# Residue-ordered keys and value rows, all attention scores in 64 by 32 tiles, far keys one block later

## The chip, the cores and the metric

The kernel runs on one core of a Trainium2 chip. The metric is device time in microseconds (us): the median of three runs of the kernel before is 1187.13 us (1186.64 to 1187.44). One further execution was taken by the hardware profiler; its own time is 1186.35 us, and the span from its first to its last instruction is 1184.6 us.

The engines are named as in the profile: PE (matrix products), PEld (PE's loading of the stationary operand), DVE (vector), ACT (activations, copies), POOL (general), SP (issues most DMAs). SBUF is the on-chip memory of 128 partitions, PSUM the memory that PE writes.

## The reference, cut to what matters

The computation is one layer of a decoder, 1024 positions by 1024 features, in float32. An input projection feeds 8 attention heads of 64 features and 4 gated-recurrence heads; their joined output is projected and added; a gated MLP with a short convolution follows, and a last norm. The change touches the attention alone, which is three causal dilated windows whose softmax sums are merged:

```python
DILATED_PATTERNS = ((128, 1), (512, 4), (2048, 16))   # (window, dilation), n_keys = window // dilation = 128
...
valid = (dist >= 0) & (dist <= n_keys) & (blk * ATTN_BLOCK + kj - ATTN_BLOCK >= 0)   # dist counted in dilated steps
s = jnp.where(valid[None, :, None, None], s, -jnp.inf)
p = jnp.exp(s - m[..., None]); l = jnp.sum(p, axis=-1)
...
w = jnp.exp(ms - jnp.max(ms, axis=0, keepdims=True))
den = jnp.sum(w * ls, axis=0); num = jnp.sum(w[..., None] * os_, axis=0)
return (num / den[..., None])[:, :S]
```

Since the three branches share scores, a query at position i sees key j with weight c(i-j) exp(score), where c counts the branches that allow the distance: every distance up to 128, multiples of 4 up to 512, multiples of 16 up to 2048. An additive mask with log c (or a very large negative number) in front of one softmax gives the same result. Two facts shape the kernel: beyond a distance of 128 only keys with the query's own residue modulo 4 count, since every multiple of 16 is one of 4 too; within it, any key may count.

## The kernel before, in words

The sequence is cut into 8 blocks of 128 queries, `b` = 0 to 7, and the 8 heads into 4 pairs, `p`; a pair's two heads `e` lie on partitions 0-63 and 64-127. `qp` and `kp` hold queries and keys with the feature on the partition. `qk_half` writes them from PSUM (lines 570 and 571): the queries of each block in the order of their residue r modulo 4 (32 queries of residue 0, then 32 of residue 1, and so on), the keys in their natural order.

`scores(p, b)` (lines 600 to 627) computes, for each of the two heads, one PSUM bank with 128 query rows. Its last columns are the near keys: the block itself and the block before it, 256 keys (128 for b = 0), as one matmul per head with 64 feature rows and 128 queries in the stationary operand (line 610). Its first `32 * b` columns are far keys: for each residue r a matmul with 32 stationary queries (line 615) that reads every fourth key from the start of the sequence to the end of block b - 1, each key 16 bytes after the last. So the previous block's own-residue keys stand in both parts, and the mask splits the distances between them. These matmuls are in plain float32; the profile shows each as two MATMUL records, so that two matmuls per near part are "x4" and eight per far part "x16". A transpose is one record.

DVE adds the mask and takes the row minimum of the negated scores (line 622), ACT takes the exponential and the row sum (line 624), DVE the reciprocal (line 625), POOL scales the probabilities (line 626). `turn(p, b)` (lines 631 to 656) transposes them on PE: `Tn` holds the near part (line 641, copied by ACT at line 642), `Tf` the far part, in one or two pieces of 128 columns (line 649, copied by DVE into `far_t` and `tri`, lines 653 and 656). `values(p, hf)` (lines 658 to 678) multiplies half a sequence (4 blocks) of transposed probabilities with the values: near with `V` (line 669), and per residue with the far rows, a full 128 keys from `far_t` (line 674) and up to 96 keys from `tri` (line 676).

The values come out of `tok` and `two` in natural order, position on the partition. `v_evac` (line 586) scales each block of 128 positions from PSUM straight into `V` and writes it to a buffer `vd` in DRAM as well (line 587); `load_far` (line 596) reads the residue-ordered far rows back.

PE's order is the program's own, written by hand. Between the pieces of attention, `fill.run` plays matmuls of the projections (lines 460 to 463, 477 to 479, 494 to 496, 514 to 516) by a fixed credit of us, so a block is: scores of the next block, filling, turn of this block, filling. The other engines' order and the DMA queues' come from a scheduler. Weights come through a ring (`Ring`): SP loads a raw chunk (line 66 or 253), ACT rounds its high part (line 86), POOL or DVE takes the rest (line 88), and up to five raw and five split chunks are ahead of PE.

Of the kernel before, what the change touches and what calls it, by code (L numbers as in the profile page):

```python
# [10 lines left out]
F32 = mybir.dt.float32  # L11
# [6 lines left out]
P = 128  # L18
# [5 lines left out]
DH = 64  # L24
# [178 lines left out]
def hybrid_kernel(ctx: ExitStack, tc: tile.TileContext, xT, w_qk, w_tok, w_hg, w_out, w_up,  # L203
# [322 lines left out]
    raw = {}  # L526
    iv = None
    if True:
        FAR, NEAR = 224, 256
        nat = at.tile([P, SEQ], F32, tag="k0", name="nat", bufs=2)  # L530
        sel = at.tile([P, FAR + NEAR], F32, tag="P0", name="sel", bufs=2)
        mask = at.tile([P, FAR + NEAR], F32, name="mask")
        scratch = drv.tile([P, FAR + NEAR], F32, name="scratch")
        nat1 = at.tile([P, FAR + NEAR], F32, tag="P1", name="nat1", bufs=2)
        nc.sync.dma_start(nat1[:, 0:NEAR], amask[:, SEQ - NEAR :])
        nc.sync.dma_start(nat[0:32, 0:896], amask[0:P:4, 0:896])
        NO = -8.0 * BIG

        POOL.tensor_scalar(sel[:, FAR:], nat1[:, 0:NEAR], DH ** 0.5, 0.0, op0=ALU.mult, op1=ALU.add)
        POOL.affine_select(out=sel[:, FAR:], in_=sel[:, FAR:], compare_op=ALU.is_ge, fill=NO, base=0,  # L540
                           pattern=[[1, NEAR]], channel_multiplier=-1)
        POOL.tensor_scalar(sel[0:32, 0:FAR], nat[0:32, 0:896:4], DH ** 0.5, 0.0, op0=ALU.mult, op1=ALU.add)
        POOL.affine_select(out=sel[0:32, 0:FAR], in_=sel[0:32, 0:FAR], compare_op=ALU.is_gt, fill=NO, base=192,
                           pattern=[[-1, FAR]], channel_multiplier=1)
        nc.sync.dma_start(scratch[:, FAR:], sel[:, FAR:])
        nc.sync.dma_start(scratch[0:32, 0:FAR], sel[0:32, 0:FAR])
        for r in range(4):
            nc.sync.dma_start(mask[32 * r : 32 * r + 32, FAR:], scratch[r:P:4, FAR:])
            nc.sync.dma_start(mask[32 * r : 32 * r + 32, 0:FAR], scratch[0:32, 0:FAR])

        tri = [at.tile([P, 2, 3, P], F32, name=f"tri{i}") for i in range(2)]
        for t in tri:
            POOL.memset(t, 0.0)
        for v, n, inv in ((V_AG, 4, 1.0 / 512), (V_HG, 4, 1.0 / P), (V_G2, 8, 1.0 / DM), (V_GF, 8, 1.0 / DM)):
            pin(POOL.tensor_scalar(vec[:, v : v + n], vec[:, v : v + n], -0.5 * inv, 0.0, op0=ALU.mult, op1=ALU.add))
        qk = {}

        def by_residue(ap):
            return ap.rearrange("p (b l r) -> p b r l", l=32, r=4)

        def qk_half(h, hf, last, tag="mm"):
            t = halves[hf]
            p, r0 = h // 2, 64 * (h % 2)

            def evac(ps):
                if p not in qk:
                    qk[p] = [at.tile([P, SEQ], F32, tag=x, name=f"{x}{p}", bufs=2) for x in ("qp", "kp")]
                qp, kp = qk[p]
                q4 = qp[r0 : r0 + 64, t].rearrange("p (b r l) -> p b r l", r=4, l=32)
                DVE.tensor_mul(q4, by_residue(ps[0:64]), by_residue(R1[0:64, t]))  # L570
                DVE.tensor_mul(kp[r0 : r0 + 64, t], ps[64:128], R1[64:128, t])
            return dense(("qk", h), hf, evac, last, tag)

        def qk_block(h):
# [5 lines left out]
        def v_evac(g):  # L580
            def evac(t, ps):
                nonlocal V
                if V is None:
                    V = vtile([P, 8, NH, DH], F32, "V")
                dst = V[:, t, 4 * g : 4 * g + 4]
                ACT.mul(dst, ps[:, :256].rearrange("p (h e) -> p h e", h=4), R1T[:, t : t + 1])
                nc.scalar.dma_start(vd[t * P : (t + 1) * P, 256 * g : 256 * g + 256], dst)
            return evac

        far_v = {}  # L590
# [9 lines left out]
        def scores(p, b):  # L600

            qp, kp = qk[p]
            far = 32 * b
            near = P if b == 0 else 2 * P
            k0 = (b + 1) * P - near
            n = far + near
            S = [bank("s", f"S{p}_{b}_{e}") for e in range(2)]
            rows = [slice(64 * e, 64 * e + 64) for e in range(2)]
            for e in range(2):
                PE.matmul(S[e][:, far:n], qp[rows[e], b * P : (b + 1) * P], kp[rows[e], k0 : k0 + near],  # L610
                          start=True, stop=True)
            for r in range(4 if b else 0):
                o = slice(32 * r, 32 * r + 32)
                for e in range(2):
                    PE.matmul(S[e][o, 0:far], qp[rows[e], b * P + 32 * r : b * P + 32 * r + 32],  # L615
                              kp[rows[e], r : r + 4 * far : 4], start=True, stop=True)
            m = mask[:, FAR - far :] if b else mask[:, FAR + P :]
            Ps = probs[p, b] = []
            for e in range(2):
                Pt = at.tile([P, FAR + NEAR], F32, tag=f"P{e}", name=f"P{p}_{b}_{e}", bufs=2)  # L620
                st = at.tile([P, 16], F32, tag="st", name=f"st{p}_{b}_{e}", bufs=8)
                DVE.tensor_tensor_reduce(Pt[:, :n], S[e][:, :n], m, -(DH ** -0.5), BIG * 3,  # L622
                                         op0=ALU.add, op1=ALU.min, accum_out=st[:, 0:1])
                ACT.activation(Pt[:, :n], Pt[:, :n], AF.Exp, bias=st[:, 0:1], scale=-1.0, accum_out=st[:, 2:3])  # L624
                DVE.reciprocal(st[:, 3:4], st[:, 2:3])  # L625
                POOL.tensor_scalar(Pt[:, :n], Pt[:, :n], st[:, 3:4], 1.0, op0=ALU.mult, op1=ALU.mult)  # L626
                Ps.append(Pt)

        near_t, far_t = {}, {}

        def turn(p, b):

            Ps = probs.pop((p, b))
            far = 32 * b
            T = bank("t", f"Tn{p}_{b}").rearrange("p (e x q) -> p e x q", e=2, x=2)
            d = near_t[p, b] = at.tile([P, 2, 2, P], F32, tag="pl", name=f"pl{p}_{b}", bufs=5)
            x0 = 0 if b else 1
            for e in range(2):
                for x in range(x0, 2):
                    c = far + (x - x0) * P  # L640
                    PE.transpose(T[:, e, x], Ps[e][:, c : c + P], ident)
            ACT.copy(d[:, :, x0:], T[:, :, x0:])
            if not b:
                return
            T = bank("t", f"Tf{p}_{b}").rearrange("p (x e q) -> p x e q", e=2, x=2)
            parts = 1 + (b > 4)
            for x in range(parts):
                for e in range(2):
                    PE.transpose(T[:, x, e], Ps[e][:, x * P : (x + 1) * P], ident)
            if b == 4:  # L650
                far_t[p] = at.tile([P, 2, 4, P], F32, tag="k0", name=f"k0_{p}", bufs=2)
            if b >= 4:
                DVE.tensor_copy(far_t[p][:, :, b - 4], T[:, 0])
            if b != 4:
                n = 32 * (b % 4)
                DVE.tensor_copy(tri[b // 4][0:n, :, b % 4 - 1], T[0:n, parts - 1])

        def values(p, hf):

# [10 lines left out]
            for r in range(4):  # L670
                q = slice(32 * r, 32 * r + 32)
                if hf:
                    for e in range(2):
                        PE.matmul(O4[rows[e], :, q], v[:, 0, r, rows[e]], far_t[p][:, e, :, q], start=False, stop=False)
                for e in range(2):
                    PE.matmul(O4[rows[e], 1:, q], v[0:96, hf, r, rows[e]], tri[hf][0:96, e, :, q], start=False, stop=(r == 3))
            DVE.tensor_copy(raw[p, hf].rearrange("p (b l r) -> p b l r", l=32, r=4),
                            O.rearrange("p (b r l) -> p b l r", r=4, l=32))

# [857 lines left out]
```

## Time and profile before

| | before |
|---|---|
| median of 3 runs | 1187.13 us |
| profiled execution, its own time | 1186.35 us |
| its span | 1184.6 us |
| PE busy | 1174.0 us, 6422 matmul records |
| DVE, ACT, POOL busy | 866.8, 563.3, 277.1 us |
| mean granted PE clock | 0.998 |
| the stretch with the attention, 36 to 265 us | 229 us, PE busy 228.94 |

A row of the page's groups reads: line, engine, operation, output<-inputs, shapes, count, then busy us and mean ns. A row of the timeline reads: start us, length us, engine, line, operation, tiles, the tile shape of PE (rows * columns of the stationary operand), partitions x columns that stream, count of records merged into the row. Consecutive records overlap in PE's pipeline, so what a group costs is read from its start to the start of the next group, not from its length.

### The profile page before, as it was taken

The page shows a single profiled execution, that of the slowest core. Times are in us where ns is not written, and L with a number is a line of the kernel's source. Part 1 is how long each engine was busy: PE and PEld are TensorE (multiplying, and loading weights), DVE is VectorE, ACT ScalarE, POOL GpSimd, SP SyncE. Part 2 cuts the span into 40 slices and gives each one's busy share as a digit, 9 for nine tenths or more (in the row PEclk, how much of TensorE's full clock was granted, in tenths as well). Part 3 has the DMA queues.
Part 4 walks back from the last instruction along what each step waited for, and adds up shares of the span by engine and source line. Part 5 has one row for each costly group of instructions (what it writes and reads, how often), then busy time and mean ns, then how long its engine had stood idle before and what let it go on. Part 6 is the DMA issues. An engine that isn't in the chain of part 4 may idle for free.

```text
span 1184.6 us, 17883 instructions
## 1 busy us (share of the span) xinstructions
PE 1174.0 (99%) x6422; PEld 964.1 (81%) x6422; DVE 866.8 (73%) x1585; ACT 563.3 (48%) x1103; POOL 277.1 (23%) x244
## 2 busy tenths in 40 slices
PE   9999999999999999999999999999999999999996
PEld 7978787778888888888888888888888888888886
DVE  7543434235887774567998988989888878858987
ACT  8424343566666655446434334343343444444553
POOL 1125253761101035231233122232222200000000
PEclk9999999999999999999999999999999999999999
DMA  7223040332112113440213332233323277435522
GB/s 259 82 76 117 28 125 28 110 121 85 37 37 81 54 63 125 142 141 29 72 54 125 116 111 85 98 125 116 107 73 113 92 241 253 140 96 168 167 94 95
DMA packets 78985, 126.73 MB, mean 107 GB/s; under 512 B 7920, under 2 KB 25104, under 8 KB 78896
## 3 DMA queue, kind: packets, MB, share of 16 engines
q1 hardware_dynamic: 65376, 103.63, 28.0%
q10 hardware_dynamic: 13520, 21.96, 4.9%
q8 instruction: 50, 0.82, 0.3%
q14 instruction: 39, 0.32, 0.1%
HBM read 99.71 MB, written 25.85 MB: 106 GB/s over the span
## 4 chain that ended last, share of the span: by engine, by line
PE 98%; DVE 1%; DMA 0%; POOL 0%; ACT 0%; SPq 0%; issue 0%; DVEq 0%; POOLq 0%
PE p L1136 11%; PE p L1137 11%; PE p L1138 11%; PE ds L1437 3%; PE ds L1435 3%; PE ds L1436 3%; PE po L1040 2%; PE po L1042 2%; PE po L1041 2%; PE da L1437 2%; PE da L1435 2%; PE da L1436 2%; PE S L610 2%; PE S L615 1%; PE piv L514 1%; PE piv L516 1%
## 5 line engine op out<-in xcount | busy, mean ns | idle before, releaser
L88 POOL TENSOR_TENSOR wlo<-raww,whi 128x512 fp32r<-128x512 f32 x137 | 204.6, 1503 | 360.7 <-ACT whi L86 249.2
L86 ACT CAST whi<-raww 128x512 fp32r<-128x512 f32 x276 | 167.9, 617 | 208.3 <-DVE raww L120 65.1
L88 DVE TENSOR_TENSOR wlo<-raww,whi 128x512 fp32r<-128x512 f32 x140 | 101.2, 724 | 24.0 <-ACT whi L86 23.9
L86 ACT CAST whi<-r 128x512 fp32r<-128x512 f32 x70 | 43.6, 623 | 85.4 <-PE ds L1436 50.0
L622 DVE CUSTOM_DVE_ANT_0 P<-S,mask 128x128 f32<-128x128 f32 (+7 forms) x64 | 31.2, 522 | 63.9 <-PE S L615 54.3
L624 ACT ACTIVATE P<-P,st 128x128 f32<-128x128 f32 (+7 forms) x64 | 37.2, 583 | 78.3 <-DVE st L622 78.2
L1437 PE MATMUL ds<-fhi,wlo 128*128 128x512 f32 x160 | 62.3, 389 | 0.0
L1436 PE MATMUL ds<-flo,whi 128*128 128x512 f32 x160 | 62.3, 389 | 0.0
L1435 PE MATMUL ds<-fhi,whi 128*128 128x512 f32 x160 | 62.2, 389 | 0.0
L1136 PE MATMUL p<-b1h,whi 128*128 128x512 f32 x160 | 62.2, 389 | 0.0
L1137 PE MATMUL p<-b1l,whi 128*128 128x512 f32 x160 | 62.2, 389 | 0.0
L1138 PE MATMUL p<-b1h,wlo 128*128 128x512 f32 x160 | 62.2, 389 | 0.0
L88 DVE TENSOR_TENSOR wlo<-r,whi 128x512 fp32r<-128x512 f32 x70 | 48.2, 690 | 19.0 <-ACT whi L86 19.0
L626 POOL TENSOR_SCALAR P<-P,st 128x128 f32<-128x128 f32 (+7 forms) x64 | 35.7, 559 | 108.7 <-DVE st L625 103.0
L1158 DVE SCALAR_TENSOR_TENSOR cv<-g,vec,cv 128x511 f32<-128x511 f32 (+2 forms) x92 | 56.2, 616 | 4.7 <-ACT cv L1155 3.7
L1409 POOL TENSOR_TENSOR facc<-facc,sqf 128x256 f32<-128x256 f32 x2 | 1.5, 738 | 223.0 <-ACT sqf L1408 223.0
L1165 ACT ACTIVATE cv<-cv 128x512 f32<-128x512 f32 x44 | 27.8, 633 | 54.3 <-DVE cv L1158 54.3
L88 DVE TENSOR_TENSOR flo<-rawf,fhi 128x512 fp32r<-128x512 f32 x70 | 48.2, 689 | 4.0 <-ACT fhi L86 4.0
L86 ACT CAST fhi<-rawf 128x512 fp32r<-128x512 f32 x70 | 43.1, 616 | 13.3 <-PE p L1138 4.7
L1435 PE MATMUL da<-fhi,whi 128*128 128x512 f32 x120 | 46.7, 389 | 0.0
L1436 PE MATMUL da<-flo,whi 128*128 128x512 f32 x120 | 46.7, 389 | 0.0
L1437 PE MATMUL da<-fhi,wlo 128*128 128x512 f32 x120 | 46.7, 389 | 0.0
(680 smaller groups left out, 3496.5 us busy)
## 6 DMA issues: line engine op xcount, KB each, us to landing
raww<-in_w_up_dram SPq DMA_DIRECT2D x88, 256.0 KB, 2.9
raww<-in_w_tok_dram SPq DMA_DIRECT2D x52, 256.0 KB, 2.9
rawf<-spT SPq DMA_DIRECT2D x40, 256.0 KB, 2.7
r<-in_w_down_dram SPq DMA_DIRECT2D x40, 256.0 KB, 3.3
raww<-in_w_hg_dram SPq DMA_DIRECT2D x32, 256.0 KB, 2.6
raww<-in_w_out_dram SPq DMA_DIRECT2D x32, 256.0 KB, 2.6
spB<-a ACTq DMA_DIRECT2D x30, 256.0 KB, 2.1
spT<-t ACTq DMA_DIRECT2D x30, 256.0 KB, 2.0
```

What stands on the lines that cost most here:

```text
L86: self.pin(self.high(hi[:, :w], raw))
L88: self.pin(low.tensor_sub(lo[:, :w], raw, f32(hi[:, :w])))
L622: DVE.tensor_tensor_reduce(Pt[:, :n], S[e][:, :n], m, -(DH ** -0.5), BIG * 3, op0=ALU.add, op1=ALU.min, accum_out=st[:, 0:1])
L624: ACT.activation(Pt[:, :n], Pt[:, :n], AF.Exp, bias=st[:, 0:1], scale=-1.0, accum_out=st[:, 2:3])
L626: POOL.tensor_scalar(Pt[:, :n], Pt[:, :n], st[:, 3:4], 1.0, op0=ALU.mult, op1=ALU.mult)
L1136: PE.matmul(ps, hi[:, s], bhi, start=(start and n == 0), stop=False)
L1137: PE.matmul(ps, hi[:, s], blo, start=False, stop=False)
L1138: PE.matmul(ps, lo[:, s], bhi, start=False, stop=(stop and n == len(rhs) - 1))
L1158: DVE.scalar_tensor_tensor(dst, x, col(V_CW + j * NFF + f), dst, op0=ALU.mult, op1=ALU.add)
L1435: PE.matmul(ps[d], hi[:, s], ahi, start=(k == 0), stop=False)
L1436: PE.matmul(ps[d], hi[:, s], alo, start=False, stop=False)
L1437: PE.matmul(ps[d], lo[:, s], ahi, start=False, stop=(k == NPAIR - 1))
```

## The change

Keys are now written in residue order inside each block too, by a second strided product on DVE (line 571 before). All scores are computed in tiles of 64 rows by 32 stationary columns: the near part is four matmuls per head, one for each residue of the queries, each streaming the same 256 keys, which lie next to each other; the far part streams runs of 32 adjacent keys, one run per block. The far part ends a block earlier, with `32 * (b - 1)` columns: blocks 0 and 1 have none, and the previous block's keys of every distance are now in the near part. So the mask is copied without the two selections on POOL, its near columns are brought into residue order, its far part is 192 columns wide instead of 224, and `tri` covers 2 blocks of a half instead of 3 (64 streamed columns instead of 96).

Since the near keys are in residue order, the rows of `V` must be. `v_evac` now scales into a small buffer `vx` (two of them), writes that to `vd`, and four DMAs on SP for each block and group of heads read the 32 rows of one residue each into `V`: 64 DMAs that were not there. `far_t` is one tile for all pairs, whose last 32 partitions are zeroed once, since block 4 now has 96 far columns.

```diff
-        FAR, NEAR = 224, 256
+        FAR, NEAR = 192, 256
...
-        POOL.affine_select(out=sel[:, FAR:], in_=sel[:, FAR:], compare_op=ALU.is_ge, fill=NO, base=0,
-                           pattern=[[1, NEAR]], channel_multiplier=-1)
...
+        POOL.tensor_scalar(in_order(sel[:, FAR:]), by_residue(nat1[:, 0:NEAR]), DH ** 0.5, 0.0, op0=ALU.mult, op1=ALU.add)
...
-        tri = [at.tile([P, 2, 3, P], F32, name=f"tri{i}") for i in range(2)]
+        tri = [at.tile([P, 2, 2, P], F32, name=f"tri{i}") for i in range(2)]
...
-                q4 = qp[r0 : r0 + 64, t].rearrange("p (b r l) -> p b r l", r=4, l=32)
-                DVE.tensor_mul(q4, by_residue(ps[0:64]), by_residue(R1[0:64, t]))
-                DVE.tensor_mul(kp[r0 : r0 + 64, t], ps[64:128], R1[64:128, t])
+                for dst, y in ((qp, slice(0, 64)), (kp, slice(64, 128))):
+                    DVE.tensor_mul(in_order(dst[r0 : r0 + 64, t]), by_residue(ps[y]), by_residue(R1[y, t]))
...
-                dst = V[:, t, 4 * g : 4 * g + 4]
-                ACT.mul(dst, ps[:, :256].rearrange("p (h e) -> p h e", h=4), R1T[:, t : t + 1])
-                nc.scalar.dma_start(vd[t * P : (t + 1) * P, 256 * g : 256 * g + 256], dst)
+                x = at.tile([P, 256], F32, tag="vx", name=f"vx{g}_{t}", bufs=2)
+                ACT.mul(x, ps[:, :256], R1T[:, t : t + 1])
+                rows = vd[t * P : (t + 1) * P, 256 * g : 256 * g + 256]
+                nc.scalar.dma_start(rows, x)
+                dst = V[:, t, 4 * g : 4 * g + 4].rearrange("p h e -> p (h e)")
+                for r in range(4):
+                    nc.sync.dma_start(dst[32 * r : 32 * r + 32], rows.rearrange("(l r) e -> r l e", r=4)[r])
...
-            far = 32 * b
+            far = 32 * max(b - 1, 0)
...
-            for e in range(2):
-                PE.matmul(S[e][:, far:n], qp[rows[e], b * P : (b + 1) * P], kp[rows[e], k0 : k0 + near],
-                          start=True, stop=True)
-            for r in range(4 if b else 0):
-                o = slice(32 * r, 32 * r + 32)
-                for e in range(2):
-                    PE.matmul(S[e][o, 0:far], qp[rows[e], b * P + 32 * r : b * P + 32 * r + 32],
-                              kp[rows[e], r : r + 4 * far : 4], start=True, stop=True)
+            k4 = kp.rearrange("p (b r l) -> p r b l", r=4, l=32)
+            for part in range(2 if far else 1):
+                for r in range(4):
+                    o = slice(32 * r, 32 * r + 32)
+                    for e in range(2):
+                        q = qp[rows[e], b * P + 32 * r : b * P + 32 * r + 32]
+                        if part == 0:
+                            PE.matmul(S[e][o, far:n], q, kp[rows[e], k0 : k0 + near], start=True, stop=True)
+                        else:
+                            PE.matmul(S[e][o, 0:far].rearrange("p (b l) -> p b l", l=32), q,
+                                      k4[rows[e], r, 0 : b - 1], start=True, stop=True)
...
-            if not b:
+            if not far:
                 return
...
-            parts = 1 + (b > 4)
+            parts = 1 + (far > P)
...
-                    PE.matmul(O4[rows[e], 1:, q], v[0:96, hf, r, rows[e]], tri[hf][0:96, e, :, q], start=False, stop=(r == 3))
+                    PE.matmul(O4[rows[e], 2:, q], v[0:96, hf, r, rows[e]], tri[hf][0:96, e, :, q], start=False, stop=(r == 3))
```

What the change does to PE's order is seen at `scores(0, 2)`, between two matmuls of a value projection (`pV`). Rows read line, operation, output<-inputs, shape of the output. Before, one matmul per head for the near keys (128 query rows, 256 columns) and then four pairs for the far keys (32 rows, 64 columns), of which the first pair is shown:

```order
L477 MATMUL pV_6_666<-whi_363,uhi 128x256
L478 MATMUL pV_6_666<-wlo_364,uhi 128x256
L479 MATMUL pV_6_666<-whi_363,ulo 128x256
L610 MATMUL S_2_0_688<-kp_335,qp_334 128x256
L610 MATMUL S_2_1_689<-kp_335,qp_334 128x256
L615 MATMUL S_2_0_688<-kp_335,qp_334 32x64
L615 MATMUL S_2_1_689<-kp_335,qp_334 32x64
```

Now there are four pairs for the near keys and four for the far keys, the first pair of each shown:

```order
L477 MATMUL pV_6_694<-whi_357,uhi 128x256
L478 MATMUL pV_6_694<-wlo_358,uhi 128x256
L479 MATMUL pV_6_694<-whi_357,ulo 128x256
L617 MATMUL S_2_0_716<-kp_329,qp_328 32x256
L617 MATMUL S_2_1_717<-kp_329,qp_328 32x256
...
L619 MATMUL S_2_0_716<-kp_329,qp_328 32x32
L619 MATMUL S_2_1_717<-kp_329,qp_328 32x32
```

The place between the same projection matmuls is kept; ten score matmuls become sixteen, all with 32 stationary columns, and the far ones stream half as many columns at this block.

SP's queue around the values of the second group of heads, before (`raww` are raw chunks of weights, `vs` the far value rows of `load_far`):

```order
L66 DMA raww_1288<-in_w_qk_dram 128x512
L66 DMA raww_1300<-in_w_tok_dram 128x512
L66 DMA raww_1448<-in_w_tok_dram 128x512
L66 DMA raww_1490<-in_w_tok_dram 128x512
L66 DMA raww_1633<-in_w_tok_dram 128x512
L66 DMA raww_1687<-in_w_tok_dram 128x512
L66 DMA raww_1767<-in_w_tok_dram 128x512
L596 DMA vs_1814<-vd 128x4x128
```

And now, where `V<-vd` are the new reads, four for each block:

```order
L588 DMA V<-vd 32x256 x4
L66 DMA raww_1377<-in_w_qk_dram 128x512
L66 DMA raww_1389<-in_w_tok_dram 128x512
L66 DMA raww_1542<-in_w_tok_dram 128x512
L588 DMA V<-vd 32x256 x8
L66 DMA raww_1590<-in_w_tok_dram 128x512
L66 DMA raww_1745<-in_w_tok_dram 128x512
L66 DMA raww_1804<-in_w_tok_dram 128x512
L588 DMA V<-vd 32x256 x4
L66 DMA raww_1892<-in_w_tok_dram 128x512
L597 DMA vs_1939<-vd 128x4x128
```

The same weight loads stand in the same order, with the reads of the blocks between them.

More of the change, by code (lines that the diff above doesn't have):

```diff
@@ L528, in hybrid_kernel, with by_residue, in_order @@
     if True:
-        FAR, NEAR = 224, 256
+        FAR, NEAR = 192, 256
+        def by_residue(ap):
+            return ap.rearrange("p (b l r) -> p b r l", l=32, r=4)
+        def in_order(ap):
+            return ap.rearrange("p (b r l) -> p b r l", l=32, r=4)
         nat = at.tile([P, SEQ], F32, tag="k0", name="nat", bufs=2)
@@ L535, in hybrid_kernel @@
         nc.sync.dma_start(nat1[:, 0:NEAR], amask[:, SEQ - NEAR :])
-        nc.sync.dma_start(nat[0:32, 0:896], amask[0:P:4, 0:896])
-        NO = -8.0 * BIG
-        POOL.tensor_scalar(sel[:, FAR:], nat1[:, 0:NEAR], DH ** 0.5, 0.0, op0=ALU.mult, op1=ALU.add)
-        POOL.affine_select(out=sel[:, FAR:], in_=sel[:, FAR:], compare_op=ALU.is_ge, fill=NO, base=0,
-                           pattern=[[1, NEAR]], channel_multiplier=-1)
-        POOL.tensor_scalar(sel[0:32, 0:FAR], nat[0:32, 0:896:4], DH ** 0.5, 0.0, op0=ALU.mult, op1=ALU.add)
-        POOL.affine_select(out=sel[0:32, 0:FAR], in_=sel[0:32, 0:FAR], compare_op=ALU.is_gt, fill=NO, base=192,
-                           pattern=[[-1, FAR]], channel_multiplier=1)
+        nc.sync.dma_start(nat[0:32, 0:768], amask[0:P:4, 0:768])
+        POOL.tensor_scalar(in_order(sel[:, FAR:]), by_residue(nat1[:, 0:NEAR]), DH ** 0.5, 0.0, op0=ALU.mult, op1=ALU.add)
+        POOL.tensor_scalar(sel[0:32, 0:FAR], nat[0:32, 0:768:4], DH ** 0.5, 0.0, op0=ALU.mult, op1=ALU.add)
         nc.sync.dma_start(scratch[:, FAR:], sel[:, FAR:])
@@ L556, in hybrid_kernel @@
         qk = {}
-        def by_residue(ap):
-            return ap.rearrange("p (b l r) -> p b r l", l=32, r=4)
         def qk_half(h, hf, last, tag="mm"):
@@ L627, in scores @@
                 Ps.append(Pt)
-        near_t, far_t = {}, {}
+        near_t = {}
+        far_t = None
         def turn(p, b):
+            nonlocal far_t
             Ps = probs.pop((p, b))
-            far = 32 * b
+            far = 32 * max(b - 1, 0)
             T = bank("t", f"Tn{p}_{b}").rearrange("p (e x q) -> p e x q", e=2, x=2)
@@ L649, in turn @@
                     PE.transpose(T[:, x, e], Ps[e][:, x * P : (x + 1) * P], ident)
-            if b == 4:
-                far_t[p] = at.tile([P, 2, 4, P], F32, tag="k0", name=f"k0_{p}", bufs=2)
             if b >= 4:
[L653 to L656, printed above, removed]
+                if far_t is None:
+                    far_t = at.tile([P, 2, 4, P], F32, tag="k0", name="far_t", bufs=2)
+                    POOL.memset(far_t[96:P], 0.0)
+                n = min(far, P)
+                DVE.tensor_copy(far_t[0:n, :, b - 4], T[0:n, 0])
+            if b % 4 >= 2:
+                n = 32 * (b % 4 - 1)
+                DVE.tensor_copy(tri[b // 4][0:n, :, b % 4 - 2], T[0:n, parts - 1])
         def values(p, hf):
@@ L673, in values @@
                     for e in range(2):
-                        PE.matmul(O4[rows[e], :, q], v[:, 0, r, rows[e]], far_t[p][:, e, :, q], start=False, stop=False)
+                        PE.matmul(O4[rows[e], :, q], v[:, 0, r, rows[e]], far_t[:, e, :, q], start=False, stop=False)
                 for e in range(2):
-                    PE.matmul(O4[rows[e], 1:, q], v[0:96, hf, r, rows[e]], tri[hf][0:96, e, :, q], start=False, stop=(r == 3))
+                    PE.matmul(O4[rows[e], 2:, q], v[0:96, hf, r, rows[e]], tri[hf][0:96, e, :, q], start=False, stop=(r == 3))
             DVE.tensor_copy(raw[p, hf].rearrange("p (b l r) -> p b l r", l=32, r=4),
```

## The prediction

> **What bounds the kernel now.** I read the page's busy times and its chain of work first, then the list of PE's waits, then the stretch of the attention.
>
> ```profile
> PE 1174.0 (99%) x6422; PEld 964.1 (81%) x6422; DVE 866.8 (73%) x1585; ACT 563.3 (48%) x1103; POOL 277.1 (23%) x244
> PE 98%; DVE 1%; DMA 0%; POOL 0%; ACT 0%; SPq 0%; issue 0%; DVEq 0%; POOLq 0%
> ...
> PE warm L383 <- DVE ones L229: 1.1, 1, 1.1
> PE p__qk___1_0_250 L460 <- ACT tw L86: 0.2, 1, 0.2
> ...
> 36.00:265.00 229.00, 228.94 (x1935) 178.29 (x1935) 91.79 (x272) 100.86 (x240) 101.77 (x115) 1.00 0.28 84
> ```
>
> PE is the chain: 98% of it. Its whole list of waits is two rows, 1.3 us. In the attention (36 to 265 us) PE is busy for 228.94 of 229 us at the full clock, while DVE, ACT and POOL (the next three) stand at 92 to 102. So the time is PE's, and a change counts by how much sooner PE can start its next matmul. A busy PE is not a fast PE, though: what one group costs has to be read from start to start.
>
> ```profile
> 207.40 0.70 PE L610 MATMUL S<-kp,qp 64*128 64x256 f32 x4
> 208.03 1.00 PE L615 MATMUL S<-kp,qp 64*32 64x224 f32 x16
> 208.96 0.50 PE L514 MATMUL piv<-whi,uhi 128*128 128x512 f32 x1
> ...
> 214.19 0.49 PE L610 MATMUL S<-kp,qp 64*128 64x128 f32 x4
> 214.62 0.50 PE L514 MATMUL piv<-whi,uhi 128*128 128x512 f32 x1
> ...
> 223.30 0.70 PE L610 MATMUL S<-kp,qp 64*128 64x256 f32 x4
> 223.93 0.33 PE L615 MATMUL S<-kp,qp 64*32 64x32 f32 x16
> 224.19 0.50 PE L514 MATMUL piv<-whi,uhi 128*128 128x512 f32 x1
> ```
>
> These are the scores of b = 7, 0 and 1. Near takes 0.63 us (207.40 to 208.03), far 0.93 us with 224 columns and 0.26 with 32; b = 0 takes 0.43, b = 1 0.89, b = 7 1.56. Far is a straight line: (0.93 - 0.26) / 192 columns / 2 records = **1.74 ns a column**, and a constant of 0.26 - 2 x 32 x 0.00174 = 0.15 us. The near rows give (0.63 - 0.43) / 128 / 2 = **0.78 ns a column**. So a far column costs twice a near one. Are its eight tiles served one after another?
>
> ```profile
> 208.09:208.13 0.04, 0.04 (x8) 0.04 (x16) 1.00 0.00 0
> 208.13:208.47 0.34, 0.34 (x16) 0.08 (x16) 1.00 0.41 96
> ```
>
> No: in the first 0.04 us of that far part eight matmul records (all of one round) are in flight, and the second round starts at the end of the second stretch. The eight run together, each at 1.74 ns. All eight read every fourth float; the near ones read neighbours.
>
> **The change part by part.** *Scores.* The open price is the rate at which eight 64 by 32 tiles stream adjacent keys. The nearest rows with several column tiles are the value products, where two tiles of 64 columns stream different adjacent data from the same 128 partitions:
>
> ```profile
> 221.65 0.39 PE L674 MATMUL O<-k,vs 128*64 128x128 f32 x4
> 221.87 0.34 PE L676 MATMUL O<-tri,vs 96*64 96x96 f32 x4
> 222.04 0.39 PE L674 MATMUL O<-k,vs 128*64 128x128 f32 x4
> ...
> 204.79 0.60 PE L649 MATMUL Tf<-ident,P 128*128 128x128 f32 x4
> 205.14 0.47 PE L514 MATMUL piv<-whi,uhi 128*128 128x512 f32 x1
> ...
> 232.37 0.38 PE L649 MATMUL Tf<-ident,P 128*128 128x128 f32 x2
> 232.51 0.48 PE L514 MATMUL piv<-whi,uhi 128*128 128x512 f32 x1
> ```
>
> Four records of 128 columns, two pairs, take 0.22 us: 0.22 / 2 / 128 = 0.86 ns. Sharing the partitions between two column tiles costs next to nothing. The bounds for four column tiles are therefore 0.78 ns (near today) and 1.74 ns (far today, if the number of tiles and not the step of 16 bytes doubles it). A gain below 0.78 is excluded, since no float32 row here is faster. I take 0.83, the middle of the adjacent rows, because the new streams are adjacent like those, and because two tiles did not slow each other at all, while a common limit would have to start exactly between two and four.
>
> The Trainium skill, "Advanced Engine Details and Errata", section SBUF Cachelines, says that SBUF is read in lines of 16 bytes and that at least two hits on a line are needed to hide its latency: a step of four floats has one hit on each line, adjacent floats four. The trace agrees with both (1.74 against 0.78 ns); by that rule the streams run at the near rate, which is the sum below.
>
> Now 2 records x (256 + 32(b - 1)) columns x 0.83 ns + 0.15 us for b of 1 to 7, and 2 x 128 x 0.83 + 0.15 = 0.36 us for b = 0. The columns for b = 1 to 7 add up to 2464: 7 x 0.15 + 2 x 2464 x 0.00083 = 5.14 us, plus 0.02 because the round of 32 columns at b = 2 (0.03 us) can't be shorter than its eight starts. Before: the straight line gives 7 x (0.89 + 1.56) / 2 = 8.58, and 0.43. So a pair costs 5.52 instead of 9.01 us, four pairs 22.1 instead of 36.0: **-13.9 us**. At 0.78 it is 1.0 more, at 0.86 it is 0.6 less, at 1.74 it is a loss of 5.0.
>
> *Transposes.* Block 1 has no far transposes (2 fewer) and block 5 needs 2 instead of 4. Four take 0.35 us and two 0.14, so two cost 0.21: 2 x 0.21 x 4 pairs = **-1.7 us**.
>
> *Far values.* `tri` streams 64 columns instead of 96. Four records went from 0.22 us at 128 columns to 0.17 at 96; the next 32 are worth the same 0.05. There are 4 residues x 8 halves = 32 such groups: **-1.6 us** (0 if weight loading sets the pace below 96 columns, though at 96 it did not).
>
> *What is added beside PE* costs nothing while it is covered.
>
> ```profile
> 29.52 1.07 DVE L570 TENSOR_TENSOR qp<-p__qk___0_0_236,R 64x512 f32<-64x512 f32 x1
> 30.59 0.69 DVE L571 TENSOR_TENSOR kp<-p__qk___0_0_236,R 64x512 f32<-64x512 f32 x1
> ...
> 207.13 0.64 POOL L626 TENSOR_SCALAR P<-P,st 128x448 f32<-128x448 f32 x1
> 211.14 0.38 PE L641 MATMUL Tn<-ident,P 128*128 128x128 f32 x2
> ...
> 22.53 1.73 SPq L548 DMA_DIRECT2D mask<-scratch  x4
> DMA to landing us min/median/max: 1.7/1.7/4.0
> 92.01 10.78 SPq L66 DMA_DIRECT2D raww<-in_w_qk_dram  x4
> 113.39 0.43 PE p__qk___4_0_1366 L460
> ```
>
> The keys' product on DVE goes from 0.69 to 1.07 us like the queries': 16 x 0.38 = 6 us on an engine that is 40% busy here (91.79 of 229). The chain from scores to transposes keeps its cover: at its tightest (pair 2, b = 6) POOL is done at 207.77 and PE comes to the transposes at 211.14, 3.4 us later; a block shortened by 0.3 to 0.7 us leaves that. `far_t` is written again for the next pair four blocks after its last reader.
>
> On SP, four reads of 32 rows (the mask's, 1.73 us of issue) stand for the four new reads of a block of V: 16 x 1.73 = 28 us of SP. The first of four waits until the block's write to `vd` has landed, 1.7 us after issue (the landing row is that write's); behind it stand weight loads, for whose splitting ACT and POOL wait. The hold-up is at most about 0.5 + 0.3 + 1.7 + 1.7 = 4.2 us (scaling, issue, landing, reads), and the weights have more: those of head 4 were issued from 92.01 to 102.8 and first used at 113.39. The cover is used up only where a block of V meets an empty ring; then PE would lose up to 4 us once. I add nothing.
>
> **Sum:** -13.9 - 1.7 - 1.6 = -17.2 us on the profiled execution's own 1186.35 us, which gives 1169.2. The median of the runs stands 0.8 above it: **1170 us**.
>
> **The rivals.** *A, four streams share one limit.* Then adjacency does not help, the price stays 1.74 ns, and near, now in 32-column tiles, pays it too: 4 x (8 x 0.15 + 0.02 + 2 x 2592 x 0.00174) = 41.0 us of scores instead of 36.0, +5.0 - 3.3 = +1.7: 1189. For it: far is the only row with four column tiles, and step and tile count change together there. Against it: the two-tile rows.
>
> *B, slower.* The near part's four tiles of a head read the same 256 keys a few ns apart, which no matmul here did. If equal addresses are served in turn, a column costs up to 4 x 0.83 = 3.3 ns. It decides from 1.78 ns a column on (4 x (1.22 + 5.184 x 1.78) = 41.8 us of scores, +2.5 in all); at 2.0 it is 4 x 11.59 = 46.4, +7.1 us: 1194; at 3.3 1221. Against it: the far tiles read the same 16 bytes on four tiles today, and stay at 1.74.
>
> *C, a partial limit.* Four adjacent streams at, say, 1.2 ns: 4 x (1.22 + 6.22) = 29.8 us, -6.2 - 3.3: 1178. Or each start costs: there are 896 score records instead of 576, and the shortest far part bounds a start by 0.26 / 16 = 0.016 us: at most 320 x 0.016 = 5.1 us, 1175. The Trainium skill, "TensorEngine Tiling (Array Packing)", section Performance Considerations, puts about 60 cycles on each matmul; at the 2.4 GHz of its "TensorE: Matmul & The Clock Gate" (the table at its head) that is an estimate of 25 ns each, 8 us for 320, and 1178. The eight records in flight within 0.04 us disagree.
>
> That the change does not do what it says is excluded by the order: near and far stand there as 32-column matmuls.
>
> **How the numbers follow.** This kernel can tell 0.2% (2.4 us) from no change. The forecast has 0.70, with its own range of 1167 to 1173 (0.78 to 0.86 ns a column, far values worth 0 to 1.6, a ring met empty once). C has 0.13 (1174 to 1181, faster still), A 0.09 (within 0.2%), B 0.08 (slower). So faster 0.83, same 0.09, slower 0.08; 1167 to 1180 leaves out B, A and a rest of C, about 0.2.
>
> **What would show it.** Right: a b = 7 score group of about 0.9 us from its first start to the next projection matmul, b = 1 about 0.57; near and far columns at one price; two transposes fewer at b = 1 and 5; PE's list of waits still near 1 us; the attention stretch 17 us shorter and every later stage as long as before. A fails or holds by one number, the ns a column of the far part: 1.74 again means shared streams. B shows as a near part above 1 us. Wrong otherwise: waits of PE on `V` or on `wlo` behind SP's new reads, or on `P` because DVE fell behind.

## The result, and the profile after

The changed kernel takes 1170.03 us (median of four runs, 1169.9 to 1170.49) where the kernel before takes 1186.89 beside it: a ratio of 0.9859, 95% interval 0.9842 to 0.9876. The forecast was 1170.0, in a range of 1167 to 1180. The profiled execution of the changed kernel takes 1170.49 us, with a span of 1168.7, so the span is 15.9 us shorter.

The page's busy times and chain, PE's list of waits and the windows of the attention, as they answer to those shown of before:

```profile
PE 1157.9 (99%) x6726; PEld 959.6 (82%) x6726; DVE 869.0 (74%) x1577; ACT 560.1 (48%) x1103; POOL 273.6 (23%) x243
PE 97%; issue 1%; DVE 1%; DMA 0%; POOL 0%; SPq 0%; ACT 0%; DVEq 0%; POOLq 0%
...
PE warm L383 <- DVE ones L229: 1.1, 1, 1.1
PE p L1146 <- POOL wlo L88: 0.4, 1, 0.4
...
36.00:248.00 212.00, 212.00 (x2237) 173.60 (x2236) 92.70 (x263) 99.31 (x240) 99.97 (x115) 1.00 0.33 99
```

PE is still the chain and is busy without a gap through the attention, which needs 17 us less. DVE spends as long in 212 us as it did in 229. One wait is new: 0.4 us for a split weight chunk (`wlo`), in a stage far behind the attention.

The timeline of PE at the scores of b = 7 (pair 2) and b = 1 (pair 3), and at a far value product of the later half:

```profile
195.48 0.66 PE L617 MATMUL S<-kp,qp 64*32 64x256 f32 x16
195.94 0.53 PE L619 MATMUL S<-kp,qp 64*32 64x192 f32 x16
196.40 0.50 PE L514 MATMUL piv<-whi,uhi 128*128 128x512 f32 x1
...
210.46 0.66 PE L617 MATMUL S<-kp,qp 64*32 64x256 f32 x16
211.05 0.50 PE L514 MATMUL piv<-whi,uhi 128*128 128x512 f32 x1
...
209.01 0.39 PE L682 MATMUL O<-far_t,vs 128*64 128x128 f32 x4
209.23 0.29 PE L684 MATMUL O<-tri,vs 96*64 96x64 f32 x4
209.34 0.39 PE L682 MATMUL O<-far_t,vs 128*64 128x128 f32 x4
```

From first start to the next projection matmul, b = 7 takes 0.92 us (1.56 before) and b = 1 0.59 (0.89); b = 0, not shown, 0.38 (0.43). The near part ahead of a far part takes 0.46 us instead of 0.63. A `tri` group takes 0.11 us (209.23 to 209.34), where it took 0.17.

Added up over the trace, where records can be told apart to the nanosecond: the 32 score groups take 22.72 us instead of 36.05 (-13.33). From the first score matmul to the first matmul of the next stage (`hf`) it is 220.46 us instead of 237.36, -16.90; 16 transposes fewer are worth -1.77, the 32 shorter `tri` groups -1.61, and the last -0.2 lies in the projection matmuls between them. Against the first matmul of the program the gain is 17.04 us when the attention ends, and 15.94 at the end: 1.1 us goes again in three small steps much later, of which the largest, 0.67 us, is at the new wait.

### The profile page after: what moved, and what is told of

Same layout as the page of the kernel before. It is cut to its first block, busy times and chain, and to the rows that moved or that the text cites. A ratio compares the mean times of both kernels' runs of the same rounds, so it can differ in the third digit from the quotient of the medians.

```text
span 1168.7 us, 18589 instructions
## 1 busy us (share of the span) xinstructions
PE 1157.9 (99%) x6726; PEld 959.6 (82%) x6726; DVE 869.0 (74%) x1577; ACT 560.1 (48%) x1103; POOL 273.6 (23%) x243
## 4 chain that ended last, share of the span: by engine, by line
PE 97%; issue 1%; DVE 1%; DMA 0%; POOL 0%; SPq 0%; ACT 0%; DVEq 0%; POOLq 0%
PE p L1146 10%; PE p L1144 10%; PE p L1145 10%; PE ds L1444 3%; PE ds L1445 3%; PE ds L1443 3%; PE po L1048 3%; PE po L1050 2%; PE po L1049 2%; PE da L1444 2%; PE da L1445 2%; PE da L1443 2%; PE S L617 2%; PE piv L514 1%; PE piv L516 1%
```

## The experiments

Three undo one part of the change each, one does a part alone on the kernel before, and one is the changed kernel again as their neighbour; then the price of a column, the cover of the added work, and the order inside a group are tried. Where a stretch "from the first score matmul to `hf`" is given, it is the difference of those two starts in that kernel's trace; it holds the attention and leaves out what chance does later.

**The changed kernel again.** No edit.

> The changed kernel once more, as the neighbour of the three that follow. My theory (adjacent keys stream at 0.83 ns a column in any number of tiles, and the later stages are as before but for chance): 1170 us, score groups of 0.92 us at b = 7 and 0.59 at b = 1. It also tests whether the 0.67 us that PE waited for a split weight chunk near 617 us in the first profile comes again: if it is the change's doing it stands there again at the same place, if it is one DMA's late landing it does not, and the span is about 0.7 us shorter.

Measured: 1169.44 us (1169.27 to 1171.0), ratio to before 0.9866 (0.985 to 0.9883); the attention stretch 220.46 us again. The wait near 617 us is not in the list of PE's waits; of the 0.67 us lost there in the first profile, 0.30 is lost again. The span is 1.3 us shorter, of which 0.6 lies in the late stages and 0.7 ahead of the first score matmul. In the first profile the wait began with one late weight chunk. First the kernel before, with the chunk's issue on SP and its first reading by DVE, then the same two rows of the changed kernel and PE's wait (in brackets: idle time before the row, and what ended it):

```profile
625.12 0.33 SPq L66 DMA_DIRECT2D raww<-in_w_up_dram  x1
628.15 0.69 DVE L115 TENSOR_TENSOR raww<-raww,raww 128x512 f32<-128x512 f32 x1 [0.86 <-DMA raww<-in_w_up_dram]
```

```profile
608.25 0.33 SPq L66 DMA_DIRECT2D raww<-in_w_up_dram  x1
612.39 0.69 DVE L115 TENSOR_TENSOR raww<-raww,raww 128x512 f32<-128x512 f32 x1 [1.97 <-DMA raww<-in_w_up_dram]
617.31 0.50 PE L1146 MATMUL p<-b12h,wlo 128*128 128x512 f32 x1 [0.40 <-POOL wlo L88]
```

The same chunk was there 3.0 us after its issue before, and 4.1 us after it here. From the first `p` matmul to the first `da` matmul, the stage that holds this wait, it is 380.9 us before, 381.6 in the first profile of the changed kernel, 381.2 in this one, and 382.0, 381.6 and 380.9 in the kernels with near keys wide, every fourth key and the longer far part. The kernel before with narrow near keys, which has none of the new reads, takes 382.0, and the changed kernel without its work beside PE 380.9. A loss of 0 to 1.1 us that comes and goes among kernels whose code is the same there is not the change's doing.

**Near keys wide again.** Undone: four 64 by 32 matmuls per head become one of 64 by 128.

```diff
-            for part in range(2 if far else 1):
-                ...
-                        if part == 0:
-                            PE.matmul(S[e][o, far:n], q, kp[rows[e], k0 : k0 + near], start=True, stop=True)
+            for e in range(2):
+                PE.matmul(S[e][:, far:n], qp[rows[e], b * P : (b + 1) * P], kp[rows[e], k0 : k0 + near],
+                          start=True, stop=True)
```

> Undoes one part: the near keys are again one matmul of 64 rows by 128 stationary columns per head, on adjacent keys; far keys stay adjacent and in 64 by 32 tiles. From the two traces, near costs 0.633 us ahead of a far part in the wide form and 0.456 in the narrow (24 groups), and 0.04 more where it stands alone (8 groups): +4.6 us, 1174.6. Rival, 'the narrow tiles earn nothing by themselves, the far keys' adjacency is all of it': no change, 1170.

Measured: 1174.74 us (1174.48 to 1175.26), +5.3 beside its neighbour; the attention stretch +5.30, the score groups +5.15. The timeline at b = 7:

```profile
198.19 0.70 PE L612 MATMUL S<-kp,qp 64*128 64x256 f32 x4
198.82 0.56 PE L617 MATMUL S<-kp,qp 64*32 64x192 f32 x16
199.31 0.49 PE L514 MATMUL piv<-whi,uhi 128*128 128x512 f32 x1
```

Near is back at 0.63 us, and the far part, unchanged in itself, takes 0.49 instead of 0.46: both together are 0.20 us a group, not the 0.177 that I expected. (Why the far part takes longer behind a wide near part is seen in the last experiment.) The narrow tiles earn 5 us of the gain by themselves, which the prediction's sum held, but under one price with the far part.

**Near keys narrow, on the kernel before.** The same part, done alone: keys in natural order, far keys at every fourth.

```diff
-            for e in range(2):
-                PE.matmul(S[e][:, far:n], qp[rows[e], b * P : (b + 1) * P], kp[rows[e], k0 : k0 + near],
-                          start=True, stop=True)
+            for r in range(4):
+                o = slice(32 * r, 32 * r + 32)
+                for e in range(2):
+                    PE.matmul(S[e][o, far:n], qp[rows[e], b * P + 32 * r : b * P + 32 * r + 32], kp[rows[e], k0 : k0 + near],
+                              start=True, stop=True)
```

> One part of the change done alone on the kernel before: near keys in four 64 by 32 tiles per head, on keys in their natural order; nothing else moves. If the gain of the narrow tiles needs nothing else, near costs 0.456 us ahead of a far part instead of 0.633 (28 groups) and 0.04 less at b = 0 (4 groups): -5.1 us, 1181.5 beside 1186.5. If it needs the far part in the same order of keys, or part of it is the later stages' chance, the attention stretch is shorter by less than 4 us.

Measured: 1181.43 us (1180.99 to 1182.22) beside 1186.42 before, ratio 0.9955 (0.9938 to 0.9972); the attention stretch -5.31. At b = 6 of pair 2 the near part takes 0.46 us:

```profile
196.45 0.66 PE L612 MATMUL S<-kp,qp 64*32 64x256 f32 x16
196.91 0.92 PE L617 MATMUL S<-kp,qp 64*32 64x192 f32 x16
```

So this third of the gain needs neither the new order of keys nor the reads of `V`.

**Every fourth key again.** Undone: the far matmuls read with the old step, in the new tiles and the new length.

```diff
-                            PE.matmul(S[e][o, 0:far].rearrange("p (b l) -> p b l", l=32), q,
-                                      k4[rows[e], r, 0 : b - 1], start=True, stop=True)
+                            PE.matmul(S[e][o, 0:far], q, kp[rows[e], r : r + 4 * far : 4], start=True, stop=True)
```

> Undoes one part: the far matmuls read every fourth key of the sequence again (the wrong keys, since these now lie in residue order, so the far scores are wrong numbers), same count, same columns, same tiles. Step theory: 1.74 instead of 0.83 ns a column, 672 columns x 2 records x 0.91 ns = 1.22 us for each of four pairs, +4.9 us, 1174.9, and 0.35 us a round at 192 columns. Rival, 'what counts is the number of tiles or the shorter far part': 1170 and 0.16 us a round.

Measured: 1175.39 us (1174.82 to 1176.04), +5.95 beside its neighbour, of which the attention stretch holds 5.30 and the score groups 5.08 (of the rest, the profiled executions show 0.5 us ahead of the first score matmul and 0.4 in the late stage above). The keys read are then not those that the scores need, but as many as before. Two far parts, of 64 and 160 columns:

```profile
173.02 0.44 PE L619 MATMUL S<-kp,qp 64*32 64x64 f32 x16
173.39 0.50 PE L460 MATMUL p__qk___6_1_2201<-uhi,whi 128*128 128x512 f32 x1
...
193.01 0.77 PE L619 MATMUL S<-kp,qp 64*32 64x160 f32 x16
193.71 0.50 PE L460 MATMUL p__qk___7_1_2411<-uhi,whi 128*128 128x512 f32 x1
```

(0.70 - 0.37) / 96 columns / 2 records = 1.72 ns a column; the changed kernel's far rounds rise by 0.83 ns a column (its second round starts 56 ns after the first with 64 columns and 163 with 192). Same tiles, same count, same columns: the step alone doubles the price.

**Other steps.** The kernel before, its keys read in other patterns for pairs 1 to 3; near matmuls are 64 by 128 (two tiles), far ones 64 by 32 (eight tiles).

```diff
+            KIND = {1: 1, 2: 2, 3: 3, 4: 4, 5: (2, 4), 6: (2, 8), 7: (4, 8)}
+            near_kind = KIND.get(b, 1)
+            far_kind = p if p < 3 or b < 3 else KIND[b]
...
-                              kp[rows[e], r : r + 4 * far : 4], start=True, stop=True)
+                              run(e, 0, far, far_kind), start=True, stop=True)
```

> A measurement of the disputed price in the kernel before: the near matmuls (64 rows by 128 columns, two tiles) and the far ones (64 by 32, eight tiles, all from the first key) read the keys of pairs 1 to 3 in other patterns, so the scores are wrong numbers. Near by block: every key (b = 1), every 2nd, 3rd, 4th key (b = 2, 3, 4), 2 of 4 (b = 5), 2 of 8 (b = 6), 4 of 8 (b = 7). Far by pair: every key (pair 1), every 2nd (pair 2), and in pair 3 by block as near. Theory of the 16-byte line (the Trainium skill, Advanced Engine Details and Errata, section SBUF Cachelines, wants two hits on a line): 0.83 ns a column for every pattern with two or more floats of each line (every key, every 2nd, 2 of 4, 2 of 8, 4 of 8), 1.74 for every 4th, between them for every 3rd, alike in two tiles and in eight. Rival, 'eight tiles on one line collide': near stays at 0.83 whatever the step. Rival, 'any step costs': every 2nd key at 1.74 too.

Measured, one run: 1182.66 us; what is read from it are its rows. "2 of 8" means two neighbours out of every eight keys. First pair 1, whose far parts read every key: near with every third (b = 3) and every fourth key (b = 4), then 2 of 8 (b = 6; 2 of 4 at b = 5 and 4 of 8 at b = 7 are read in the same way and not shown). Then pair 3's far parts of b = 3 (every third) and b = 4 (every fourth).

```profile
122.73 0.94 PE L621 MATMUL S<-kp,qp 64*128 64x256 f32 x4
123.60 0.40 PE L625 MATMUL S<-kp,qp 64*32 64x96 f32 x16
123.92 0.50 PE L460 MATMUL p__qk___4_1_1424<-uhi,whi 128*128 128x512 f32 x1
128.94 1.15 PE L621 MATMUL S<-kp,qp 64*128 64x256 f32 x4
130.02 0.45 PE L625 MATMUL S<-kp,qp 64*32 64x128 f32 x16
130.40 0.50 PE L460 MATMUL p__qk___5_0_1509<-uhi,whi 128*128 128x512 f32 x1
...
143.83 0.73 PE L621 MATMUL S<-kp,qp 64*128 64x256 f32 x4
144.49 0.56 PE L625 MATMUL S<-kp,qp 64*32 64x192 f32 x16
...
232.31 0.48 PE L625 MATMUL S<-kp,qp 64*32 64x96 f32 x16
232.72 0.50 PE L514 MATMUL piv<-whi,uhi 128*128 128x512 f32 x1
...
238.81 0.66 PE L625 MATMUL S<-kp,qp 64*32 64x128 f32 x16
239.40 0.50 PE L514 MATMUL piv<-whi,uhi 128*128 128x512 f32 x1
```

Near with every key takes 0.63 us (the before's rows). Every third adds 0.24 us, every fourth 0.45, 2 of 4 0.02, 2 of 8 0.03, 4 of 8 nothing; divided by 512 (256 columns, two records) and added to 0.83 that is 1.30, 1.71, 0.87, 0.89 and 0.83 ns a column. Eight tiles agree (to the nanosecond in the trace): every third takes 409 instead of 325 ns at 96 columns (+0.44 ns, 1.27), every fourth 593 instead of 379 at 128 (+0.84, 1.67). Every second key adds 19 ns to two records of 256 columns in two tiles, and 19 to two of 224 in eight: 0.87. (In pair 3, b = 1 and 2 also read every third.) So the number of tiles has no part in it, and a step as such has none. Neighbouring keys of one feature lie four bytes apart, four in a line of 16 bytes, so a column needs a quarter of a line (every key, 4 of 8), a half (every second, 2 of 4, 2 of 8), three quarters (every third) or a whole one (every fourth). The measured prices are close to the larger of 0.83 and about 1.72 ns times that share: 0.83, 0.86, 1.29, 1.72. Lines of 8 or of 32 bytes don't fit: with 8, every second key would cost as much as every fourth, and with 32, 2 of 8 would. The Trainium skill, "Advanced Engine Details and Errata", section SBUF Cachelines, says that SBUF has lines of 16 bytes and that at least two hits on a line are needed to absorb its latency; the trace agrees, with 0.87 ns at two hits, 1.27 to 1.30 between one and two, and 1.67 to 1.72 at one.

**Far part one block longer.** Undone: `far = 32 * b` in scores and transposes, with the added columns masked out.

```diff
-            far = 32 * max(b - 1, 0)
+            far = 32 * b
...
-                                      k4[rows[e], r, 0 : b - 1], start=True, stop=True)
+                                      k4[rows[e], r, 0 : b], start=True, stop=True)
```

> Undoes one part: the far part is 32 * b columns long again, so block 1 has one and block 5 needs two pieces transposed; the added columns are masked out, since the near part holds those keys, and the far value product stays at 64 columns. Scores: 32 columns x 2 x 0.83 ns = 0.053 us for each of 7 blocks and 4 pairs, +1.5; transposes: two more at b = 1 and b = 5, 0.21 us each, +1.7. Sum +3.2 us, 1173.2. Rival, 'the shorter far part is hidden behind the weight loads of the tiles': +1.7 or less, 1171.7.

Measured: 1173.18 us (1172.95 to 1173.39), +3.7; the attention stretch +3.21, as expected. At b = 7 (224 far columns) the group takes 0.97 us instead of 0.92, and each of the other blocks from b = 2 on takes 0.05 more as well (in the trace, 811 instead of 757 ns at b = 4).

**Without the work beside PE.** The keys' product in natural order, `V` written by ACT directly.

```diff
-                for dst, y in ((qp, slice(0, 64)), (kp, slice(64, 128))):
-                    DVE.tensor_mul(in_order(dst[r0 : r0 + 64, t]), by_residue(ps[y]), by_residue(R1[y, t]))
+                DVE.tensor_mul(in_order(qp[r0 : r0 + 64, t]), by_residue(ps[0:64]), by_residue(R1[0:64, t]))
+                DVE.tensor_mul(kp[r0 : r0 + 64, t], ps[64:128], R1[64:128, t])
...
-                for r in range(4):
-                    nc.sync.dma_start(dst[32 * r : 32 * r + 32], rows.rearrange("(l r) e -> r l e", r=4)[r])
```

> Takes away the work beside PE that the change added: the keys' product on DVE writes in natural order, ACT writes V directly, and the 64 reads of V on SP and the small buffer are gone. The scores and the near values are wrong numbers then (keys and mask in different orders), PE's matmuls are the same. My theory, all of it was covered: 1170 us, the attention stretch within 0.3 us, DVE 6 us less busy. Rival, 'the reads of V or DVE hold PE up somewhere': up to 4 us less, 1166.

Measured: 1168.94 us (1168.51 to 1169.21); the attention stretch 220.28 us against 220.46. The windows of the attention:

```profile
36.00:248.00 212.00, 211.99 (x2239) 173.81 (x2238) 86.78 (x264) 99.35 (x240) 100.33 (x115) 1.00 0.29 89
```

DVE has 5.9 us less to do (86.78 against 92.70) and PE gains 0.18. The cover held.

**Dearer reads of V.** Each of the 64 reads cut into four on SP; then, for a point between, into two; then the four issued by ACT.

```diff
-                    nc.sync.dma_start(dst[32 * r : 32 * r + 32], rows.rearrange("(l r) e -> r l e", r=4)[r])
+                    for c in range(0, 256, 64):
+                        nc.sync.dma_start(dst[32 * r : 32 * r + 32, c : c + 64],
+                                          rows.rearrange("(l r) e -> r l e", r=4)[r][:, c : c + 64])
```

> Makes the added reads dearer: each read of V is cut into four of 64 columns, 256 DMAs on SP instead of 64, so that a block of V takes about 16 x 0.43 = 6.9 us of SP's issue instead of 1.7. If the cover is the 10 us that the weights had in the trace, a hold-up of 4.2 + 5.2 = 9.4 us still just fits: 0 to +1 us, 1170 to 1171. Rival, 'the reads were nearly at the bound': 5 us for each of several blocks, +10 us or more, 1180.

Measured with 256 reads: 1190.57 us (1187.75 to 1192.5), 20 us lost, nearly all at one place. PE's rows and SP's rows there, and the windows around it (us, PE, PEld, DVE, ACT, POOL, granted clock):

```profile
92.27 0.27 PE L496 MATMUL pV<-whi,ulo 128*128 128x256 f32 x1
108.04 0.58 PE L494 MATMUL pV<-whi,uhi 128*128 128x256 f32 x1 [15.49 <-ACT whi L86]
...
36.86 33.32 SPq L589 DMA_DIRECT2D V<-vd  x64
...
70.88 32.00 SPq L589 DMA_DIRECT2D V<-vd  x64
...
103.55 0.56 SPq L66 DMA_DIRECT2D raww<-in_w_tok_dram  x1
...
96.00:110.00 14.00, 1.82 (x7) 1.47 (x7) 0.75 (x2) 1.24 (x2) 0.00 (x0) 0.50 0.45 123
110.00:116.00 6.00, 5.85 (x31) 5.56 (x30) 1.38 (x3) 2.46 (x5) 2.56 (x2) 0.59 0.73 239
```

SP issues the reads of the first group of heads from 36.9 us on, 128 of them at about 0.5 us each, until 102.9, and the next weight load stands behind them; PE needs that weight at 92.5. The granted clock falls to 0.50 in the wait and stays there until 114.9, 6.9 us after PE has gone on, so that 15.5 us of waiting cost 19.5. Another 1.7 us goes at 194 to 197 us, where weight loads stand behind 48 reads of the second group of heads:

```profile
PE pV L494 <- ACT whi L86: 15.5, 1, 15.5
...
PE p__qk___7_0_2480 L463 <- POOL wlo L88: 0.6, 1, 0.6
PE p__qk___7_0_2480 L460 <- ACT whi L86: 0.4, 1, 0.4
```

Together that is the 21.2 us by which the attention stretch is longer; the 1.1 us that the changed kernel's profiled execution lost in later stages is not lost here. My expectation of 0 to 1 us was wrong: I had set one block's hold-up against the cover, and the blocks' reads stand together in the queue.

> Between the changed kernel (64 reads of V, nothing lost) and the one with 256 (PE stood 15.5 us for a rounded weight at 92.5 us, while SP issued reads of V until 102.5 and only then the weight load): each read in two halves, 128 DMAs. If the loss is SP's issue time, at 0.46 us a read, the reads that ended at 102.5 end about 15 us sooner, near 88, and with landing and rounding (5.7 us there, from 103.55 to 109.29) the weight is ready near 94: a wait of 0 to 2 us, 1170 to 1172. If it is instead the landing of many small transfers, the loss stays near half of 21 us, 1180.

Measured with 128 reads, one run: 1169.51 us, no new wait, the attention stretch 220.46 us. SP's rows, and then those of the changed kernel at the same load:

```profile
53.94 16.39 SPq L589 DMA_DIRECT2D V<-vd  x32
...
71.00 1.04 SPq L66 DMA_DIRECT2D raww<-in_w_tok_dram  x2
```

```profile
52.25 5.06 SPq L588 DMA_DIRECT2D V<-vd  x8
59.64 0.36 SPq L66 DMA_DIRECT2D raww<-in_w_tok_dram  x1
```

The reads end at 70.3, not 88 as I had worked out (I had left out that the first 64 are paced by issue too), and the first weight load goes out at 71.0. With the 4.5 us from issue to PE's start seen in the kernel with 256 reads (103.55 to 108.04), a load must leave by about 88 for a use at 92.5: the spare time is some 17 us with 128 reads and some 28 with the change's 64 (59.64).

> The 256 reads again, but issued by ACT instead of SP, so that no weight load stands behind them on SP. Theory, SP's queue was the path of the loss: the 15.5 us wait for a rounded weight is gone from where the load was late; ACT pays the issue instead (256 x 0.46 = 118 us in all over two stretches), which its rounding of weights can't all hide: less than 21 us of loss, but not none, 1172 to 1185. Rival, 'the transfers themselves are in the way of the weights': the same wait at the same place, 1190.

Measured, one run: 1260.61 us, far worse than expected. The list of who waited for these issues:

```profile
L589 ACTq DMA_DIRECT2D V<-vd x256: 308/432/1706, 36.6 to 259.3; - x128
  ACT P L630: 46.0, 4
  ACT whi L86: 39.8, 4
  ACT vx L583: 34.3, 3
```

Behind the issues, and the waits for `vd` in them, stand ACT's own exponentials, roundings and scalings of the next block, 120 us of waiting in these three rows, and PE waits for those in turn. The late weight load on SP is out of the way, but this says little of the rival, since the loss on ACT hides all else.

**Far part first.** Only the order of the two parts in a group.

```diff
-            for part in range(2 if far else 1):
+            for part in (1, 0) if far else (0,):
```

> Same matmuls, the far part ahead of the near part. In the changed kernel the first round of a group takes 240 ns for 256 columns where the second takes 216. If these 24 ns belong to whichever round opens the group (its weight loads have nothing before them to hide behind), they move to the far part's first round and near's first takes 216: time unchanged, 1170. If they belong to 256 columns of near, near stays at 240 + 216. If the far rounds of 32 columns (40 ns) had hidden something behind near, the time grows by up to 24 x 0.03 = 0.7 us.

Measured: 1169.73 us (1169.09 to 1170.88); the score groups 22.73 against 22.72 us. In the trace near's first round now takes 216 ns, as its second does, and the far part's first round 187 at 192 columns where it took 163. The 24 ns belong to the round that opens a run of 64 by 32 tiles, whichever it is. A near part in wide tiles makes the far part open such a run of its own, which is the 0.02 us that it gained there.

## Why the prediction was right

**What bounds the kernel**, PE from start to start, holds: wherever PE does not wait, a kernel's attention stretch follows from the starts of its PE rows.

**Scores**, -13.9 us forecast, -13.33 measured. The price of adjacent keys in eight tiles, which I took as 0.83 ns, is 0.83. (The lower bound, 0.78, came from rows rounded to 10 ns: before the change the near part goes from 422 ns at 128 columns to 633 at 256, 0.82 ns a column. That no float32 row is faster holds for the plain float32 matmuls alone: the projections', which work on operands rounded to fp32r and are called f32 in the profile too, stream 512 columns in 0.23 us, 0.45 ns a column.) The term that was mis-sized is the constant, 0.15 us a group: it measured 0.17 (379 ns at b = 0 less 2 x 128 x 0.83 = 212; 918 at b = 7 less 2 x 448 x 0.83 = 744), and 32 x 0.02 us is the missing 0.6. I had taken it from the strided far parts, where it is 0.15 again with every fourth key; in the kernel of the other steps the same far parts with every key have 0.17 (539 ns at 224 columns less 372). So it belongs to adjacent streams in the old layout as in the new; why strided ones show 0.02 less was not taken apart. The forecasts of 0.894 us at b = 7 and 0.575 at b = 1 came out as 0.92 and 0.59.

**One price hid two causes.** The sum came out, but it did not say where the gain is. Undone one at a time, the narrow near tiles are worth 5.3 us, the adjacent far keys 5.3, the shorter far part 3.2, and `tri` 1.6 by its rows (not undone). These are 15.4 of 16.9; the rest lies between the parts: 224 columns fewer a pair at the old price are worth 0.4 us more than at the new, 1.6 for four pairs, which makes 17.0, 0.1 more than was measured.

**Transposes** (-1.7 forecast, -1.77 measured) and **far values** (-1.6, -1.61) are as worked out.

**The work beside PE** costs nothing, as forecast: without it PE gains 0.18 us in the attention. The reason given was half right. The cover of the weights holds, with some 28 us to spare at the first group of heads, but the bound of "up to 4 us once" does not follow from it: it was made for one block, and when four times as many reads, those of eight blocks together, filled the queue, 19.5 us went at one place.

**Later stages** are not exactly as long as before, as the prediction had it: 1.1 us went in them in the profiled execution, mostly with one late weight chunk, and 0.5 in the second execution of the same kernel. It and the constant are why the sum gave 1169.2 for an execution that took 1170.49. That the median fell on 1170.0 is partly luck: the sum was 1.3 us short, and the 0.8 added for the median of the runs made up for part of it; the rest came of the changed kernel's median, which stands 0.5 below its profiled execution and not above it.

**The rivals.** A (shared streams at 1.74 ns) and C's partial limit (1.2 ns) fall with the 0.83 ns in eight tiles. B (equal addresses in turn) falls too: four tiles read the same 256 keys at 216 ns for 256 columns. The price for each start falls with the near part: 16 records instead of 4 made it faster. The Trainium skill, "TensorEngine Tiling (Array Packing)", section Performance Considerations, has about 60 cycles of overhead for each matmul, from which 1178 was estimated; here the records of a round start 6 to 7 ns apart (in the trace of the changed kernel), and no such price for each record is seen in this form of tiles.

## What to carry to other kernels

Price a matmul's stream by the lines it touches: with plain float32, every second element costs nearly nothing more (0.87 ns a column instead of 0.83), every fourth doubles the price, so a layout that makes neighbours of what is read together is worth a strided write on an engine with time to spare. Undo the parts of a change one by one even when the sum fits, since a third of this gain needed none of the reordering. For work put on a queue ahead of loads, add up all that stands ahead of the load, and not one item of it.

## What had not been expected

The wide form of the near part, 64 by 128, has a gap that the narrow one lacks: 256 columns at 0.83 ns are 213 ns, and its two records start 320 ns apart (trace of the kernel with near keys wide again), while the rounds of four narrow tiles a head follow at 240 and 216. The same 107 ns stand there at b = 0, where 128 columns are 106 ns and the two records start 213 apart. What fills them was not tried.

A column's price goes up smoothly with the lines touched (0.87 ns at half a line, 1.27 to 1.30 at three quarters, 1.67 to 1.72 at one), and not in one step at two hits. And the clock, at 1.00 in the windows of the attention above, went to 0.50 in the trace 1.9 us into a wait of 15.5 us, and back to 1.00 6.9 us after its end: 4 us were lost to it besides the wait.
